# A latent attention's order written out tile by tile, and a recurrence's group norms emitted after it

## The chip, the cores and the metric

One core of one Trainium2 chip runs the whole program. The time is device microseconds of one execution, the median of three. "Before" is the kernel without the change. The engines are TensorE (PE, with its weight loads as PEld), VectorE (DVE), ScalarE (ACT), GpSimd (POOL) and SyncE (SP).

## The reference, cut to what matters

The program is two decoder layers and a further block. Each layer projects its input, runs a two-way RWKV recurrence and a latent attention on the same projection, mixes both, and runs a mixture of experts. Of a layer, the change touches these two parts (T is 1040 tokens: 16 meta tokens and 1024):

```python
# latent attention: 4 heads, 128 + 64 wide keys, 128 wide values
s = jnp.einsum('bqhd,bkhd->bhqk', qn, k_nope) + jnp.einsum('bqhd,bkd->bhqk', qp, k_pe)
p = jax.nn.softmax(s.astype(jnp.float32) * scale, axis=-1)
out = jnp.einsum('bhqk,bkhd->bqhd', p, v)
# end of the recurrence: group norm over each head of 64, bonus, gate
mu = jnp.mean(y, -1, keepdims=True)
var = jnp.mean(jnp.square(y - mu), -1, keepdims=True)
yn = ((y - mu) * lax.rsqrt(var + RWKV_GN_EPS)).reshape(B, L, RW) * gn_g + gn_b
out = (yn + (bonus_f + bonus_b).reshape(B, L, RW)) * g
```

## The kernel before, in words

Matrix products keep fp32 accuracy by splitting each operand in a high and a low half (names ending in h and l) and adding three products: `split` (L251 on ScalarE, L252 on VectorE) makes the halves, `mm3` (L256 to L258) multiplies.

**`recur`** ends with nine calls of `r_post` (L985), one for the 16 meta rows and eight for 128 rows each. A row loads four arrays from HBM, adds on GpSimd (L996), takes the mean on VectorE (L1001, L1002), subtracts on GpSimd (L1003), squares on ScalarE (L1004), sums on VectorE (L1006), takes the root on ScalarE (L1007) and the reciprocal on VectorE (L1008), multiplies and adds on GpSimd (L1009, L1010) and VectorE (L1011 to L1013), gates on GpSimd (L1014) and stores the row (L1015). `mix_out`, after the attention, reads it. ScalarE's root and exponential use different tables, each change is an `ACT_TABLE_LOAD`. Its tiles (names q_...) have two buffers each.

**`mla`** makes the halves of the latent inputs and weights, then for head h `qk` (projections of q and k, split), `qk_rotary` (the rotary part `qs`, a copy on ScalarE, L1098, and a subtraction on VectorE, L1099) and, for each pair of heads, `values`. PSUM has two large tiles (`big`, three banks each) and two of one bank (tag t). A head's 9 query tiles form four groups, [0,1,2], [3,4], [5,6], [7,8].

`scores` does one query tile: 15 matmuls (L1149), the row maximum (L1151, L1152), the exponentials with their sums (L1155, L1157), nine transposes of the probabilities `Pm` in three sets, key tiles 1 to 4, 5 to 8, and tile 0 (L1163), each set with a copy from PSUM on ScalarE (L1166), and a cast and a subtraction on VectorE (L1169, L1170) into `pth` and `ptl`. `output` multiplies a group's probabilities by the values (27 matmuls, `ops`), and copies to `m_ot` (L1179); with a head's last group it also transposes back (L1186), writes `y_att` (L1189) and squares and sums (`m_sq`, `s_ss`, L1192 to L1194).

Nothing here is in a manual order: the Tile framework's scheduler lays out each engine's instructions from the program order and its own costs, so the rows of `r_post` and the tiles of `mla` are interleaved by it on all engines. Only the loop of `recur` runs in a written order (`manual_schedule`). `mla` is called with the recurrence's work ahead of it in program order.

Of the kernel before, what the change touches and what calls it, by code (L numbers as in the profile page):

```python
# [10 lines left out]
F32 = mybir.dt.float32  # L11
# [161 lines left out]
class K:  # L173
# [521 lines left out]
    def recur(self, li, S):  # L695
        nc, tc, I = self.nc, self.tc, self.I
        with ExitStack() as es:
# [6 lines left out]
            R = dict(li=li, S=S)  # L704
# [9 lines left out]
            R.update(ap=ap, bp=bp, mp=mp, st=pool("r_s", 2), tp=pool("r_t", 2), qp=pool("q_t", 2, side="right"),  # L714
# [12 lines left out]
            qc = pool("q_c", 1, side="right")  # L727
            R["gb"] = self.bcast(qc, I["rwkv_gn_g"][li], RW, "gn_g")
            R["bb"] = self.bcast(qc, I["rwkv_gn_b"][li], RW, "gn_b")
# [71 lines left out]
            for i in range(9):  # L801
                self.r_post(R, i)
# [219 lines left out]
    def mla(self, li, p, S, Y):  # L1022
# [7 lines left out]
        with ExitStack() as es:  # L1030
# [48 lines left out]
            def qk(h):  # L1079
# [6 lines left out]
                c3(lambda q, c, n: self.split(qh[:, c:c + n], ql[:, c:c + n], ps[:, q, :n]))  # L1086
                kh = hp.tile([128, T], F32R, name="kh")
# [3 lines left out]
                return [(qh, kh), (qh, kl), (ql, kh)]  # L1091
# [10 lines left out]
            def values(pr):  # L1102
# [3 lines left out]
                wv = [w[:, pr, 1].rearrange("p h f -> p (h f)") for w in (wkh, wkl)]  # L1106
                for i, (c, n) in enumerate(TT):
                    vp = pst.tile([128, 512], F32, name="vps", tag="t")
                    self.mm3(vp[:n, :256], ckh[:, c:c + n], ckl[:, c:c + n], wv[0], wv[1], True, True)
                    self.split(vh[:n, i], vl[:n, i], vp[:n, :256])  # L1110
                return vh, vl

            QK, V = {0: qk(0)}, {0: values(0)}
            with self.tpool(name="m_r", bufs=1) as lp:
# [15 lines left out]
                for pr in range(2):  # L1130
# [5 lines left out]
                    if pr == 0:  # L1136
                        QK[0] += qk_rotary(0)
# [4 lines left out]
            def scores(h, i, terms, pth, ptl, o):  # L1142
# [4 lines left out]
                for q, (c, m) in enumerate(self.KC):  # L1147
                    for z, (l, r) in enumerate(terms):
# [5 lines left out]
                sm = S["sums"][:, h, i]  # L1154
                nc.scalar.activation(P[:n, 0:696].rearrange("p (a b) -> p a b", a=2), sp[:n, 0:2, :348], AF.Exp,  # L1155
                                     scale=rq[:n, i:i + 1], bias=mx[:n], accum_out=sm[:n, 0:1])
                nc.scalar.activation(P[:n, 696:T], sp[:n, 2, 4:348], AF.Exp, scale=rq[:n, i:i + 1], bias=mx[:n],  # L1157
                                     accum_out=sm[:n, 1:2])
                for kts in ((1, 2, 3, 4), (5, 6, 7, 8)) + ((0,),):
# [5 lines left out]
                    kn, z, k0 = TT[kts[0]][1], len(kts), TT[kts[0]][0]  # L1165
                    nc.scalar.activation(P[:kn, k0:k0 + z * n].rearrange("p (z n) -> p z n", z=z), pt[:kn, :z, :n], AF.Copy)  # L1166
# [5 lines left out]
            def output(h, ot, w0, W, pth, ptl, last):  # L1172
# [7 lines left out]
                if not last:  # L1180
                    return
# [9 lines left out]
                sq = tp.tile([128, 8, 128], F32, name="m_sq", bufs=1)  # L1191
                nc.scalar.activation(sq, rows, AF.Square)  # L1192
                nc.vector.tensor_reduce(S["ss"][:, h, 1:9], sq, AX.X, ALU.add)
                nc.scalar.activation(sq[:NM, 0], rp[:NM, 1024:1152], AF.Square, accum_out=S["ss"][:NM, h, 0:1])  # L1194

            due = None
            for h in range(4):
                ot = None
                for z, grp in enumerate(groups):
                    w0 = TT[grp[0]][0]  # L1200
                    W = TT[grp[-1]][0] + TT[grp[-1]][1] - w0
                    pth = ep.tile([128, 9, 272], F32R, name="pth")
                    ptl = ep.tile([128, 9, 272], F32R, name="ptl")
                    for i in grp:
                        scores(h, i, QK[h], pth, ptl, TT[i][0] - w0)
                    if due:
                        output(*due)
# [1315 lines left out]
```

## Time and profile before

| | us |
|---|---|
| before, median of 3 | 4390.69 |
| lowest to highest | 4386.52 to 4403.39 |
| the profiled execution | 4402.54 |
| its span | 4400.7 |
| mean granted clock, share of 2.4 GHz | 0.903 |

The span is the time between the first and the last instruction on the core. A busy time is the sum over an engine's instructions, weight loads (PEld) run beside matmuls. "Idle before" is the time in which the engine stood still ahead of an instruction, put down to what ended it.

### The profile page before, as it was taken

What the parts mean: (1) busy time and instruction counts of PE and PEld (TensorE: products, weight loads), DVE (VectorE), ACT (ScalarE), POOL (GpSimd) and SP (SyncE); (2) the same over time, 40 slices, a digit from 0 to 9 for tenths busy, and PEclk for the clock granted to TensorE, in tenths of its full rate; (3) what the DMA queues carried; (4) which work ended last, traced back from release to release, by engine and by line L of the source; (5) the groups of instructions that cost most, each with busy time, mean ns of one, the idle gap of its engine ahead of it and who ended that gap; (6) DMA issues with size and microseconds to landing.
All of it is one profiled execution on the core that took longest, in us unless ns stands there. A gap on an engine that the chain in (4) does not pass through costs nothing. (4 is left out here: it accounts for less than half of the span.)

```text
span 4400.7 us, 68329 instructions
## 1 busy us (share of the span) xinstructions
PE 3830.7 (87%) x27155; PEld 3157.1 (72%) x27155; DVE 2767.7 (63%) x4684; ACT 1869.7 (42%) x3033; POOL 988.2 (22%) x719
## 2 busy tenths in 40 slices
PE   7888897899699688897887896997898889999998
PEld 7677676786576476776776775765786677888786
DVE  7763777757698757627668577997644753333354
ACT  4323445542387543233555532876424522111232
POOL 2331124201242243311233012331422410000000
PEclk9788798999799887886988997999998899999999
DMA  4446663113499833447641043998521121111232
GB/s 154 101 129 183 160 161 108 37 54 128 160 345 346 300 102 101 115 143 172 165 125 58 1 172 131 340 335 309 181 73 29 53 97 58 48 48 43 90 126 81
DMA packets 384153, 611.94 MB, mean 139 GB/s; under 512 B 50467, under 2 KB 217602, under 8 KB 381762
## 3 DMA queue, kind: packets, MB, share of 16 engines
q1 hardware_dynamic: 278402, 485.38, 35.3%
q10 hardware_dynamic: 85200, 70.97, 5.4%
q0 software_dynamic: 20224, 51.15, 3.7%
q8 instruction: 216, 3.54, 0.3%
q14 instruction: 111, 0.91, 0.1%
HBM read 491.65 MB, written 123.45 MB: 140 GB/s over the span
## 5 line engine op out<-in xcount | busy, mean ns | idle before, releaser
L252 DVE TENSOR_TENSOR w13l<-xw,w13h 128x1024 fp32r<-128x1024 f32 x248 | 296.4, 1220 | 57.5 <-ACT w13h L251 53.9
L251 ACT ACTIVATE w13h<-xw 128x1024 fp32r<-128x1024 f32 x256 | 267.4, 1058 | 130.3 <-PE x_hp L258 76.6
L256 PE MATMUL pp_ps<-T_hi,pw_hi 128*128 128x348 f32 x912 | 309.7, 340 | 8.7 <-ACT T_hi L1752 2.9
L257 PE MATMUL pp_ps<-T_lo,pw_hi 128*128 128x348 f32 x912 | 305.4, 335 | 1.4 <-DVE T_lo L1757 1.3
L258 PE MATMUL pp_ps<-T_hi,pw_lo 128*128 128x348 f32 x912 | 304.3, 334 | 0.0
L2414 PE MATMUL f_mm<-F_hi,f_wh 128*128 128x512 f32 x704 | 222.8, 398 | 1.7 <-ACT F_hi L251 1.7
L2414 PE MATMUL f_mm<-F_lo,f_wh 128*128 128x512 f32 x704 | 222.6, 397 | 0.0
L2414 PE MATMUL f_mm<-F_hi,f_wl 128*128 128x512 f32 x704 | 222.3, 397 | 0.0
L256 PE MATMUL x_hp<-w13h,x_h 128*96 128x512 f32 x512 | 208.5, 407 | 0.1
L257 PE MATMUL x_hp<-w13l,x_h 128*96 128x512 f32 x512 | 204.7, 400 | 0.0
L258 PE MATMUL x_hp<-w13h,x_l 128*96 128x512 f32 x512 | 204.0, 398 | 0.0
L256 PEld LDWEIGHTS pp_ps<-T_hi,pw_hi 128*128 128x128 f32 x912 | 179.8, 197 | 21.8 <-issue 7.8
L257 PEld LDWEIGHTS pp_ps<-T_lo,pw_hi 128*128 128x128 f32 x912 | 179.8, 197 | 5.1 <-DVE T_lo L1757 2.6
L287 POOL TENSOR_TENSOR g_x<-g_x,g2g 128x1024 f32<-128x1024 f32 x6 | 14.3, 2385 | 750.4 <-ACT g_x L284 750.4
L258 PEld LDWEIGHTS pp_ps<-T_hi,pw_lo 128*128 128x128 f32 x912 | 179.5, 197 | 3.0 <-issue 3.0
L252 DVE TENSOR_TENSOR f_wl<-F_raw,f_wh 128x1024 fp32r<-128x1024 f32 x44 | 53.7, 1221 | 203.2 <-ACT f_wh L251 203.2
L251 ACT ACTIVATE f_wh<-F_raw 128x1024 fp32r<-128x1024 f32 x44 | 46.4, 1060 | 307.0 <-PE f_mm L2414 301.4
L1616 POOL DMA_INDIRECT d_y<-x_o,r_idx x64 | 102.8, 1606 | 312.1 <-DVE x_al L252 288.8
L825 PE MATMUL aa<-ar_p,bk_p 64*128 64x128 f32 x1088 | 134.0, 376 | 40.2 <-DVE A L827 33.6
L2414 PEld LDWEIGHTS f_mm<-F_hi,f_wh 128*128 128x128 f32 x704 | 133.1, 189 | 34.4 <-ACT F_hi L251 2.0
L2414 PEld LDWEIGHTS f_mm<-F_lo,f_wh 128*128 128x128 f32 x704 | 132.7, 189 | 32.8 <-DVE F_lo L252 0.6
L2414 PEld LDWEIGHTS f_mm<-F_hi,f_wl 128*128 128x128 f32 x704 | 132.9, 189 | 32.4
(630 smaller groups left out, 11221.3 us busy)
## 6 DMA issues: line engine op xcount, KB each, us to landing
xw<-in_moe_w SPq DMA_DIRECT2D x256, 512.0 KB
xw<-in_moe_w SPq DMA_DIRECT2D x64, 1024.0 KB
wd_raw<-in_w_down SPq DMA_DIRECT2D x44, 512.0 KB
pw_raw<-in_w_in SPq DMA_DIRECT2D x36, 512.0 KB
d_AR<-AR ACTq DMA_DIRECT2D x32, 544.0 KB
d_BK<-BK ACTq DMA_DIRECT2D x32, 544.0 KB
ar_p<-d_AR SPq DMA_DIRECT2D x68, 256.0 KB
bk_p<-d_BK SPq DMA_DIRECT2D x68, 256.0 KB
```

Of the source, the lines that this page charges most:

```text
L251: nc.scalar.activation(hi, src, AF.Copy)
L252: (lo_eng or nc.vector).tensor_tensor(lo, src, hi.bitcast(F32), ALU.subtract)
L256: mm(out, wh, xh, start=first, stop=False)
L257: mm(out, wh, xl, start=False, stop=False)
L258: mm(out, wl, xh, start=False, stop=last)
L287: e1.tensor_tensor(out[:n], out[:n], gb[:n], ALU.mult)
L825: nc.tensor.matmul(aa[d][:, h - z], bk[q, h], ar[q, h], start=True, stop=True)
L1616: nc.gpsimd.indirect_dma_start(out=y2[:, :], out_offset=bass.IndirectOffsetOnAxis(ap=si, axis=0), in_=y, in_offset=None, bounds_check=2 * ...
L2414: nc.tensor.matmul(p[:, j], a[:, k], b[:, k, 512 * j:512 * j + 512], start=st, stop=sp)
```

## The change

`recur` no longer emits the rows: it returns nine calls, and `mla` emits them at its end, after the attention, in program order. Their pool `q_t` has one buffer for each tile instead of two and lives until the end of `mla`; the group norm's weights lie in it from the start of `recur`.

`mla` runs 36 query tiles in 38 turns under a manual order for TensorE, ScalarE and VectorE. Turn t emits the scores of tile t, the transposes and splits of tile t−1 (`turned`), the exponentials of tile t, and then an output that is due (`output`, and `back` at a head's end), a piece of `values(1)` or of the next head's `qk`. Key tile 0 comes first in `turned`, and its halves are made straight from PSUM. `m_sq` is squared and summed in two halves. The rows, emitted behind, are still placed by the scheduler: GpSimd's and SyncE's instructions are free, and it sets the rows' VectorE and ScalarE instructions into the written order.

```diff
-    def recur(self, li, S):
+    def recur(self, li, S, qs):
-            R = dict(li=li, S=S)
+            R = dict(li=li, S=S, qp=qs)
+            R["gb"] = self.bcast(qs, I["rwkv_gn_g"][li], RW, "gn_g")
+            R["bb"] = self.bcast(qs, I["rwkv_gn_b"][li], RW, "gn_b")
...
-            R.update(ap=ap, bp=bp, mp=mp, st=pool("r_s", 2), tp=pool("r_t", 2), qp=pool("q_t", 2, side="right"),
+            R.update(ap=ap, bp=bp, mp=mp, st=pool("r_s", 2), tp=pool("r_t", 2),
...
-            qc = pool("q_c", 1, side="right")
-            R["gb"] = self.bcast(qc, I["rwkv_gn_g"][li], RW, "gn_g")
-            R["bb"] = self.bcast(qc, I["rwkv_gn_b"][li], RW, "gn_b")
...
-            for i in range(9):
-                self.r_post(R, i)
+            return iter([lambda i=i: self.r_post(R, i) for i in range(9)])
...
-    def mla(self, li, p, S, Y):
+    def mla(self, li, p, S, Y, rows):
...
+                yield None
...
-                return [(qh, kh), (qh, kl), (ql, kh)]
+                yield None
+                yield [(qh, kh), (qh, kl), (ql, kh)] + qk_rotary(h)
...
+                    if i in (4, 8):
+                        yield
+            QK, V = {}, {}
+            Q = qk(0)
+            for z in range(2):
+                next(Q)
+            for z in values(0):
+                pass
...
-                        QK[0] += qk_rotary(0)
+                        QK[0] = next(Q)
...
-            def scores(h, i, terms, pth, ptl, o):
+            def scores(h, i, terms):
...
+                def exps():
+                    sm = S["sums"][:, h, i]
+                    nc.scalar.activation(P[:n, 0:696].rearrange("p (a b) -> p a b", a=2), sp[:n, 0:2, :348], AF.Exp,
+                                         scale=rq[:n, i:i + 1], bias=mx[:n], accum_out=sm[:n, 0:1])
+                    nc.scalar.activation(P[:n, 696:T], sp[:n, 2, 4:348], AF.Exp, scale=rq[:n, i:i + 1], bias=mx[:n],
+                                         accum_out=sm[:n, 1:2])
+                return P, exps
-                for kts in ((1, 2, 3, 4), (5, 6, 7, 8)) + ((0,),):
+            def turned(P, i, pth, ptl, o):
+                n = TT[i][1]
+                for kts in ((0,), (1, 2, 3, 4), (5, 6, 7, 8)):
                     pt = pst.tile([128, 4, 128], F32, name="ptp", tag="t")
                     for z, kt in enumerate(kts):
                         kc, kn = TT[kt]
                         nc.tensor.transpose(pt[:kn, z, :n], P[:n, kc:kc + kn], self.ident[:n, :n])
                     kn, z, k0 = TT[kts[0]][1], len(kts), TT[kts[0]][0]
+                    if z == 1:
+                        ph, pl = pth[:kn, 0, o:o + n], ptl[:kn, 0, o:o + n]
+                        nc.scalar.activation(ph, pt[:kn, 0, :n], AF.Copy)
+                        nc.vector.tensor_tensor(pl, pt[:kn, 0, :n], ph.bitcast(F32), ALU.subtract)
+                        continue
...
-            def output(h, ot, w0, W, pth, ptl, last):
+            def output(h, ot, w0, W, pth, ptl):
...
-                if not last:
-                    return
+            def back(h, ot):
...
-                sq = tp.tile([128, 8, 128], F32, name="m_sq", bufs=1)
-                nc.scalar.activation(sq, rows, AF.Square)
-                nc.vector.tensor_reduce(S["ss"][:, h, 1:9], sq, AX.X, ALU.add)
+                sq = tp.tile([128, 4, 128], F32, name="m_sq", bufs=1)
+                for z in (0, 4):
+                    nc.scalar.activation(sq, rows[:, z:z + 4], AF.Square)
+                    nc.vector.tensor_reduce(S["ss"][:, h, 1 + z:5 + z], sq, AX.X, ALU.add)
...
-            due = None
-            for h in range(4):
-                ot = None
-                for z, grp in enumerate(groups):
-                    w0 = TT[grp[0]][0]
-                    W = TT[grp[-1]][0] + TT[grp[-1]][1] - w0
-                    pth = ep.tile([128, 9, 272], F32R, name="pth")
-                    ptl = ep.tile([128, 9, 272], F32R, name="ptl")
-                    for i in grp:
-                        scores(h, i, QK[h], pth, ptl, TT[i][0] - w0)
-                    if due:
-                        output(*due)
-                    if h == 2 and z == 0:
-                        V[1] = values(1)
-                    if z == 0:
-                        ot = tp.tile([128, T], F32, name="m_ot", bufs=1)
-                    if z == 1 and h < 3:
-                        QK[h + 1] = qk(h + 1) + qk_rotary(h + 1)
-                    due = (h, ot, w0, W, pth, ptl, z == 3)
-            output(*due)
+            jobs = [(h, z, i) for h in range(4) for z, grp in enumerate(groups) for i in grp]
+            ot, cur, due, prev, value = None, None, [], None, iter(())
+            with self.tc.manual_schedule(engines={mybir.EngineType.PE, mybir.EngineType.Activation, mybir.EngineType.DVE}):
+                for t in range(len(jobs) + 3):
+                    exps = None
+                    if t < len(jobs):
+                        h, z, i = jobs[t]
+                        P, exps = scores(h, i, QK[h])
+                    now, done = due, []
+                    due = []
+                    if prev:
+                        Pp, (hp_, zp, ip) = prev
+                        grp = groups[zp]
+                        if ip == grp[0]:
+                            w0 = TT[ip][0]
+                            W = TT[grp[-1]][0] + TT[grp[-1]][1] - w0
+                            if zp == 0:
+                                ot = tp.tile([128, T], F32, name="m_ot", bufs=1)
+                            cur = [ep.tile([128, 9, 272], F32R, name=nm) for nm in ("pth", "ptl")]
+                        turned(Pp, ip, *cur, TT[ip][0] - w0)
+                        if ip == grp[-1]:
+                            due = [(hp_, ot, w0, W, *cur)]
+                            last = zp == 3
+                    if exps:
+                        exps()
+                    for job in now:
+                        output(*job)
+                        if job[0] == 1 and job[2] == TT[7][0]:
+                            value = values(1)
+                        if job[2] == TT[7][0]:
+                            back(*job[:2])
+                    next(value, None)
+                    if t < len(jobs):
+                        if h < 3 and z == 1 and i == groups[1][0]:
+                            Q = qk(h + 1)
+                        if h < 3 and (z, i) in ((1, groups[1][0]), (1, groups[1][1]), (2, groups[2][0])):
+                            got = next(Q)
+                            if got:
+                                QK[h + 1] = got
+                        prev = (P, jobs[t])
+                    else:
+                        prev = None
+            for row in rows:
+                row()
...
-                self.recur(li, S)
+                qs = ExitStack()
+                rows = self.recur(li, S, qs.enter_context(self.tpool(name="q_t", bufs=1)))
...
-                    self.mla(li, p, S, Y)
+                    self.mla(li, p, S, Y, rows)
+                    qs.close()
```

The order of instructions shows it at three places. First TensorE, early in layer 0's loop, where transposes (`ptp`) and score matmuls (`ms`) meet. Before:

```order
L1163 MATMUL ptp<-ident,Pm 16x16
L1163 MATMUL ptp<-ident,Pm 128x128 x4
L1149 MATMUL ms<-kh,qh 128x348
L1149 MATMUL ms<-kl,qh 128x348
L1149 MATMUL ms<-kh,ql 128x348
L1149 MATMUL ms<-kph,qs 128x348
L1149 MATMUL ms<-kpl,qs 128x348
L1163 MATMUL ptp<-ident,Pm 128x128 x4
L1163 MATMUL ptp<-ident,Pm 16x128
L1149 MATMUL ms<-kh,qh 128x348
```

Now, in a turn whose output (`ops`) follows:

```order
L1157 MATMUL ms<-kh,ql 128x348
L1157 MATMUL ms<-kph,qs 128x348
L1157 MATMUL ms<-kpl,qs 128x348
L1178 MATMUL ptp<-ident,Pm 16x128
L1178 MATMUL ptp<-ident,Pm 128x128 x8
L256 MATMUL ops<-pth,vh 128x272
L257 MATMUL ops<-ptl,vh 128x272
```

The score matmuls that lay between the transposes of the first and the second four key tiles are gone; nine transposes follow each other, tile 0 first, and the output follows them.

Second VectorE, at the start of layer 0's loop (`qs` is the rotary part of q, `q_...` are the rows). Before:

```order
L1012 TENSOR_TENSOR q_y_6782<-q_y_6782,gn_g 128x512
L1099 TENSOR_TENSOR qs<-qpe_7016,qs 64x1040
L1134 TENSOR_TENSOR qr<-ms,sin 128x348
L1134 TENSOR_TENSOR qr<-ms,sin 128x346 x2
L1013 TENSOR_TENSOR q_y_6782<-q_y_6782,q_v 128x512
L1099 TENSOR_TENSOR qs<-qpe_7016,qs 64x1040
L252 TENSOR_TENSOR vl<-vps,vh 128x256
L1151 TENSOR_REDUCE mx<-ms 16x1
L1151 TENSOR_REDUCE mx<-ms 128x1
L1152 TENSOR_TENSOR mx<-mx,s_nrq 16x1
L1152 TENSOR_TENSOR mx<-mx,s_nrq 128x1
L1001 TENSOR_REDUCE q_mu<-q_y_6807 128x8
```

Now:

```order
L1100 TENSOR_TENSOR qs<-qpe_6786,qs 64x1040
L1142 TENSOR_TENSOR qr<-ms,sin 128x348
L1142 TENSOR_TENSOR qr<-ms,sin 128x346 x2
L252 TENSOR_TENSOR vl<-vps,vh 128x256
L1159 TENSOR_REDUCE mx<-ms 16x1
L1160 TENSOR_TENSOR mx<-mx,s_nrq 16x1
L1159 TENSOR_REDUCE mx<-ms 128x1
L1160 TENSOR_TENSOR mx<-mx,s_nrq 128x1
L1185 TENSOR_TENSOR ptl<-ptp,pth 16x16
L1190 CAST pth<-Pm 128x4x16
```

The second `qs`, which is head 1's, has left the place ahead of the first maxima `mx`; so has the row of 128 that stood there.

Third ScalarE, at the first row inside the loop. Before:

```order
L1166 ACTIVATE Pm<-ptp 128x64 x2
L1004 ACTIVATE q_y_6808<-q_y_6807 128x512
L1007 ACT_TABLE_LOAD
L1007 ACTIVATE q_vr<-q_vr,eps_gn 128x8
L1166 ACTIVATE Pm<-ptp 16x16
L1166 ACTIVATE Pm<-ptp 128x512
L1155 ACT_TABLE_LOAD
L1155 ACTIVATE Pm,s_sums<-ms,mx,s_rq 128x696
L1157 ACTIVATE Pm,s_sums<-ms,mx,s_rq 128x344
L1166 ACTIVATE Pm<-ptp 128x512
```

Now:

```order
L1184 ACTIVATE pth<-ptp 16x16
L1187 ACTIVATE Pm<-ptp 128x64 x2
L1165 ACTIVATE Pm,s_sums<-ms,mx,s_rq 128x696
L1167 ACTIVATE Pm,s_sums<-ms,mx,s_rq 128x344
L1003 ACTIVATE q_y_9355<-q_y_9354 128x512
L1184 ACTIVATE pth<-ptp 16x128
L1187 ACTIVATE Pm<-ptp 128x512 x2
L1006 ACT_TABLE_LOAD
L1006 ACTIVATE q_vr<-q_vr,eps_gn 128x8
L1165 ACT_TABLE_LOAD
L1165 ACTIVATE Pm,s_sums<-ms,mx,s_rq 128x696
L1167 ACTIVATE Pm,s_sums<-ms,mx,s_rq 128x344
```

A row's square (`q_y`) and root (`q_vr`) still lie between copies and exponentials, with two table loads for it; the copies of one tile now stand together.

## Rows read from the trace of the kernel before

**Rows 1.** The page's first part: busy us (share of the span) and instructions.

```profile
PE 3830.7 (87%) x27155; PEld 3157.1 (72%) x27155; DVE 2767.7 (63%) x4684; ACT 1869.7 (42%) x3033; POOL 988.2 (22%) x719
```

**Rows 2.** Timeline, layer 0: start us, us, operation, idle before it.

```profile
710.80 0.32 PE L1149 MATMUL ms<-kh,qh 128*16 128x348 f32 x1 [1.10 <-DVE qpe L1134]
715.36 6.93 DVE L1099 TENSOR_TENSOR qs<-qpe,qs 64x1040 fp32r<-64x1040 f32 x1
722.66 2.37 DVE L1151 TENSOR_REDUCE mx<-ms 16x1 f32<-16x1044 f32 x2
725.18 1.28 ACT L1155 ACT_TABLE_LOAD   x1 [13.98 <-DVE mx L1152]
727.55 1.11 PE L1163 MATMUL ptp<-ident,Pm 16*128 16x16 f32 x8 [8.96 <-ACT Pm L1155]
...
841.85 1.25 DVE L1151 TENSOR_REDUCE mx<-ms 128x1 f32<-128x1044 f32 x1 [0.31 <-PE ms L1149]
...
995.14 0.19 ACT L1194 ACTIVATION_READ_ACCUMULATOR m_sq<-ms 16x1 f32 x1
```

**Rows 3.** Timeline, layer 1: first score matmul, last square.

```profile
2279.05 0.32 PE L1149 MATMUL ms<-kh,qh 128*16 128x348 f32 x1
...
2554.28 0.19 ACT L1194 ACTIVATION_READ_ACCUMULATOR m_sq<-ms 16x1 f32 x1
```

**Rows 4.** Tile `mx`, layers 0 and 1: duration ns min/median/max, first, last start.

```profile
L1151 DVE TENSOR_REDUCE mx<-ms x36: 1222/1245/1247, 722.7 to 972.6; 128x1 f32<-128x1044 f32 x32, 16x1 f32<-16x1044 f32 x4
L1151 DVE TENSOR_REDUCE mx<-ms x36: 1225/1245/1247, 2286.4 to 2533.3; 128x1 f32<-128x1044 f32 x32, 16x1 f32<-16x1044 f32 x4
```

**Rows 5.** Table of stretches: us; engines' busy us; clock; DMA share; GB/s.

```profile
680.00:710.00 30.00, 23.64 (x126) 23.09 (x126) 24.61 (x42) 15.03 (x28) 11.54 (x11) 0.83 0.45 136
728.00:842.00 114.00, 92.25 (x517) 83.89 (x516) 92.10 (x170) 70.86 (x146) 46.92 (x41) 0.83 0.23 65
842.00:973.00 131.00, 117.21 (x782) 105.94 (x782) 79.94 (x178) 70.18 (x175) 0.74 (x2) 0.96 0.00 1
973.00:997.00 24.00, 17.54 (x117) 14.67 (x114) 11.02 (x28) 10.75 (x23) 0.66 (x4) 0.91 0.85 294
2306.00:2410.00 104.00, 77.61 (x469) 69.44 (x468) 83.70 (x152) 60.75 (x125) 46.92 (x36) 0.89 0.22 66
```

**Rows 6.** Groups by line, 842 to 973 us: busy us, mean ns; idle before.

```profile
L1151 DVE TENSOR_REDUCE mx<-ms 128x1 f32<-128x1044 f32 x20 | 24.9, 1244 | 17.3 <-PE ms L1149 17.1
L1166 ACT ACTIVATE Pm<-ptp 128x512 f32<-128x512 f32 x35 | 19.9, 593 | 20.8 <-PE ptp L1163 20.6
L1169 DVE CAST pth<-Pm 128x512 fp32r<-128x512 f32 x34 | 14.2, 419 | 15.7 <-ACT Pm L1166 15.3
```

**Rows 7.** Waits, 842 to 973 us: engine, line, releaser: us, times, longest.

```profile
DVE ql L252 <- ACT qh L251: 2.5, 1, 2.5
PE ptp L1163 <- ACT Pm L1166: 2.5, 7, 1.1
PE ops L256 <- ACT Pm L1166: 2.2, 6, 0.6
```

**Rows 8.** Groups by line, 728 to 842 us, VectorE, ScalarE, GpSimd in turn.

```profile
L1169 DVE CAST pth<-Pm 128x512 fp32r<-128x512 f32 x24 | 14.9, 636 | 3.2 <-ACT Pm L1166 3.1
L1011 DVE TENSOR_TENSOR q_y<-q_y,q_vr 128x512 f32<-128x512 f32 x7 | 5.5, 788 | 0.1
L1008 DVE RECIPROCAL q_vr<-q_vr 128x8 f32<-128x8 f32 x7 | 1.4, 196 | 3.1 <-ACT q_vr L1007 3.1
...
L1007 ACT ACT_TABLE_LOAD x7 | 9.0, 1283 | 0.8 <-POOL q_y L1014 0.7
L1004 ACT ACTIVATE q_y<-q_y 128x512 f32<-128x512 f32 x7 | 4.4, 623 | 4.4 <-POOL q_y L1003 4.4
...
L1014 POOL TENSOR_TENSOR q_y<-q_y,q_g 128x512 f32<-128x512 f32 x7 | 10.1, 1442 | 20.3 <-DVE q_y L1013 16.6 <-DVE q_mu L1002 3.7
L995 POOL DMA_DIRECT2D q_y<-d_y x11 | 7.0, 635 | 13.1 <-DVE q_vr L1006 9.6 <-DMA d_yr<-q_y 3.5
```

More of the change, by code (lines that the diff above doesn't have):

```diff
@@ L1106, in values @@
                 wv = [w[:, pr, 1].rearrange("p h f -> p (h f)") for w in (wkh, wkl)]
+                V[pr] = vh, vl
                 for i, (c, n) in enumerate(TT):
@@ L1110, in values @@
                     self.split(vh[:n, i], vl[:n, i], vp[:n, :256])
-                return vh, vl
-            QK, V = {0: qk(0)}, {0: values(0)}
+                    if i in (4, 8):
[6 more added lines that the diff above has]
+                pass
             with self.tpool(name="m_r", bufs=1) as lp:
@@ L1153, in scores @@
                 P = tp.tile([128, T], F32, name="Pm", bufs=3)
[L1154 to L1158, printed above, removed]
-                for kts in ((1, 2, 3, 4), (5, 6, 7, 8)) + ((0,),):
+                def exps():
[8 more added lines that the diff above has]
+                for kts in ((0,), (1, 2, 3, 4), (5, 6, 7, 8)):
                     pt = pst.tile([128, 4, 128], F32, name="ptp", tag="t")
```

## The prediction

> **What bounds the kernel now.** I read the page's first part, then the table of stretches, then the instructions of one tile, then the waits. TensorE is busy 87% of the span [rows 1], and the change touches only the attention `mla` and the last nine steps of the recurrence, twice each (two layers). So everything is read from those two places. The timeline's first score matmul and the last square of layer 0 stand at 710.80 and 995.14, those of layer 1 at 2279.05 and 2554.28 [rows 2, 3]: 284.5 and 275.4 us, 6.5 and 6.3% of the span.
>
> Inside these stretches there are three regimes. First a start: from the first score matmul to the first row maximum (722.66 in layer 0, 2286.36 in layer 1) 11.9 and 7.3 us pass. Then 35 intervals between the first and the last of 36 row maxima, 250.0 us to 972.6 and 246.9 us to 2533.28 [rows 3, 4]. Then a tail of 22.7 and 21.2 us. In the middle the table of stretches [rows 5] splits: 842 to 973 us holds no group norms: 20 full maxima [rows 6] and two short ones, whose 21 intervals take 130.8 us (from 841.85 [rows 2] to 972.6), 6.23 us a tile, with TensorE busy 117.21 of 131 us and VectorE 79.94. 728 to 842 us holds seven group-norm rows and only 14 intervals in 119.2 us, 8.5 us a tile, with TensorE at 92.25 of 114 and VectorE at 92.10. Layer 1's stretch of the second kind, 2306 to 2410 us, reads like layer 0's. So without group norms TensorE is the limit and waits little; with them all engines share a tangle.
>
> The start of layer 0 has a stall of its own [rows 2]: VectorE's second `qs` (head 1's) takes 6.93 us while GpSimd works; behind it stand `vl` and the first two row maxima, ScalarE then sits 13.98 us before its table load and TensorE 8.96 us before the first transposes.
>
> **The change, part by part.** I price TensorE's chain, since in the new order it is the engine that every iteration comes back to.
>
> *Fixed order without group norms.* TensorE's own work per tile stays: 117.21 us over 21 tiles are 5.58 us. What changes is what it waits for. Now one iteration is 15 score matmuls, nine transposes, perhaps an output. Before, score matmuls of a later tile lay between the transposes of key tiles 1 to 4 and those of 5 to 8, as the printed order shows; now nothing does, and the second four need the PSUM tile that ScalarE's copy of the first four must have left. That copy takes 593 ns [rows 6], and it stands behind the copy of the 16-row tile. Before, this kind of wait cost 2.5 us over 7 times, 0.36 on average and 1.1 at the longest [rows 7]; these are my two bounds. I take 0.9, near the longest, because with nothing between the whole chain shows: the copy's 0.59 and about 0.3, an estimate between that and the 1.1, for the last transpose to come out and the copy to start. In an iteration with an output, its first matmul waits in the same way for the copy of key tiles 5 to 8; before 2.2 us in 6 times, 0.6 at the longest [rows 7]. There are 16 outputs for 36 tiles, so I add 0.9 × 16/36 = 0.4. The projections of heads 1 to 3 now go in as three pieces each, and ScalarE's and VectorE's halves of their splits alternate: the row before has VectorE waiting 2.5 us for the first of them [rows 7], and I take 3.7 for a head's set, 11 us over 36 tiles or 0.3. Sum: 5.58 + 0.9 + 0.4 + 0.3 = 7.2 us a tile against 6.23. VectorE's work (79.94 us over 22 tiles, 3.6 a tile) and ScalarE's (70.18, 3.2) [rows 5] fit under that, so neither is the bound; the cast of the 16-row key tile that goes from VectorE counts nothing there.
>
> *Group norms.* The same nine rows come with the same instructions and their place in the loop hardly moves: row 0 before it, rows 1 to 8 inside (before rows 0 and 1 stood ahead). One row's price on VectorE is seven steps, from 788 ns (`q_y` by `q_vr`) to 196 ns (the reciprocal), 3.95 us together; on ScalarE a square of 0.62 and two table loads of 1.283, 3.2 us [rows 8]. Lower bound 0 (it falls into their idle time); upper bound 7.1 (one after the other on the path). I take 2.6, the two table loads, because they are ahead of exponentials that TensorE's next transposes need: 8 × 2.6 = 21 us. To this come 4 us for VectorE running slower beside GpSimd (a large cast takes 636 ns there [rows 8] and 419 without it [rows 6]: 5 us for 24 casts, most of it in the path). Sum for the middle: 35 × 7.2 + 25 = 277 us, against 250 and 247: +27 and +30.
>
> *The chain of a row.* One buffer instead of two means that the loads of row i+1 wait until row i is stored. GpSimd already waits 3.5 us in all for such a store [rows 8], and SP's and GpSimd's queues carry no other work here that the loop needs before its end. So I cost the single buffer at nothing by itself; its cover is that rows stand two iterations apart, and if that goes the price is rival 2.
>
> *Start.* Head 1's `qs` moves from ahead of the loop to iteration 5, where the work of five tiles is past and the next head is four iterations off. So no long `qs` stands before the first maximum. I take 5.5 us for the start (15 short matmuls at the low clock, one wait for `qs`): −6 in layer 0, −2 in layer 1. *Ahead of the loop* VectorE is busy 24.61 of 30 us [rows 5]; row 1's seven instructions leave it, 3.95 us, and I take −4 a layer (bounds 0 and −5, since GpSimd's help ends too).
>
> *Tail.* From the last maximum: transposes 1.9 with their wait, an output 4, again transposes 1.9, an output 4, then output transposes, copy, squares in two halves, about 6: 18 to 19, against 22.7 and 21.2. I take −3. The loads of `mix_out`'s weights may go out earlier, but nothing waited for them, so 0.
>
> **Sum.** Layer 0: 27 − 6 − 4 − 3 = +14; layer 1: 30 − 2 − 4 − 3 = +21; together +35, less about 4 that I allow because some of the waits fall under a row's stall anyway: +31. On the profiled execution's 4402.5 us that is 4433.5; that execution lay 11.8 us above the median 4390.7, so I predict 4390.7 + 31 = **4422**.
>
> **The clock.** TensorE was granted 0.96 of its 2.4 GHz between 842 and 973 us, but 0.83 between 728 and 842, and 0.89 in layer 1's stretch with group norms [rows 5]: there it dropped to 1.2 GHz for parts. If the new stretches without group norms came at 0.89, TensorE's 5.58 us would grow by 0.44 us, times 44 tiles 19 us more. I leave this out of the sum, since the tail shows 0.91 with many waits, and keep it for the upper end. The Trainium skill, "TensorE: Matmul & The Clock Gate", Part 1, says that the throttled state is the default and that activity releases it, which speaks against an order that makes TensorE wait in each iteration; going by it the 19 us would be due, 4441. The trace agrees in that its stretches with more waits have the lower clock, 0.83 against 0.96.
>
> **Rivals.**
> 1. *Faster: the transposes' wait stays at its old price.* If ScalarE is always free when the first four transposes come out, and weight loads of the next hide the start, the wait is the 0.36 of before and not 0.9. Over 52 waits a layer that takes off 28 us, twice 28 = 56: 4366. It would cease to be slower from a wait of 0.6. For it: 7 such waits averaged that. Against: those had matmuls of other tiles between. Chance 0.24.
> 2. *Slower by more: rows hold the queues.* If a row's VectorE or ScalarE step stands in the fixed order before its input has come from GpSimd or from a store, the whole loop stands. Speaking for it: in one such stretch VectorE waited 3.1 us for ScalarE's `q_vr`. Against: the long waits were GpSimd's, 16.6 us for VectorE's `q_y` [rows 8], so its results were early. With 5.1 us a row (half-way from the 3.1 of the sum to 7.1): 16 rows × 2.0 more is +32, 4454; at 7.1 it is 4486. The Trainium skill, "PSUM — Partial Sum Buffer", "Engine vs sequencer instructions", calls these engines' queues strict FIFO; nothing behind passes a waiting step. Chance 0.18.
> 3. *No change: the rows are hidden.* If rows fall into time in which VectorE and ScalarE idle (ScalarE was busy 70.86 of 114 us), the 25 us a layer go: 4422 − 50 = 4372. Chance 0.2. This is also where it ends if the new order is only the old one written out in effect.
>
> **How the numbers follow.** Forecast 0.38, its own range 4400 to 4445. A measurement here tells about 0.5%, 22 us, from no change: faster is under 4369, slower over 4412. Faster: 0.18 of rival 1 and 0.06 of rival 3 (both at once, or less at the clock), 0.24. Same: 0.06 of rival 1, 0.13 of rival 3, 0.11 of the forecast, 0.30. Slower: 0.27 of the forecast, 0.18 of rival 2, a rest of 0.01: 0.46. The range takes in most of rival 1 and the middle of rival 2: 4352 to 4465.
>
> **What would show it.** In the changed profile: maxima 7.2 us apart where no group norms lie; TensorE's transposes waiting for ScalarE's copy over 30 times, about 0.9 us each; the first maximum some 5.5 us behind the first score matmul; a tail of 18 to 19 us; 3 us a row on top. Maxima at most 6.6 us apart, or the rows without effect on their spacing, make the forecast wrong towards faster; a table load or `q_vr` reciprocal waiting several us in every row, towards slower.

## The result, and the profile after

The changed kernel took 4433.15 us (4426.66 to 4439.29, 4 runs) against 4388.67 for the kernel before in the same comparison: ratio 1.0094, 95% interval 1.0067 to 1.0121, 44 us more. The profiled execution took 4431.16 us with a span of 4429.3, close to that median; the one of before, 4402.54, lay above its own.

In the trace the difference lies in the two attention loops. From the first projection to the first matmul of `mix_out` layer 0 took 322.7 us, before 314.3, and layer 1 330.6, before 304.8: 34 us in all. These two stretches before, then now (the view of [rows 5]; behind a stretch's length stands TensorE's busy time with the count of its matmuls, and the third number from the end is its granted clock, a mean of time at 1.2 and at 2.4 GHz as a share of 2.4):

```profile
682.10:996.40 314.30, 257.13 (x1570) 232.26 (x1570) 220.99 (x430) 167.41 (x371) 71.06 (x64) 0.89 0.20 62
2250.80:2555.60 304.80, 248.75 (x1571) 222.59 (x1571) 214.49 (x430) 166.60 (x371) 75.53 (x64) 0.92 0.20 62
```

```profile
678.70:1001.40 322.70, 253.08 (x1571) 228.54 (x1571) 210.28 (x398) 175.28 (x377) 72.64 (x67) 0.91 0.21 66
2251.00:2581.60 330.60, 260.46 (x1571) 235.04 (x1571) 209.73 (x398) 175.12 (x377) 72.01 (x67) 0.88 0.21 65
```

The matmuls are the same but for one record. What is left of a stretch when TensorE's busy time is taken off is the time in which it stands: 57.2 and 56.1 us before, 69.6 and 70.1 now, 12.4 and 14.1 more. The busy time itself fell by 4.1 us in layer 0, where the granted clock rose from 0.89 to 0.91, and rose by 11.7 in layer 1, where the clock fell from 0.92 to 0.88. So TensorE stands longer by about the same in both layers, and that layer 1 lost 26 us and layer 0 only 8 goes with the clock.

The row maxima show where the time went; 36 of them, first and last start (the view of [rows 4]):

```profile
L1159 DVE TENSOR_REDUCE mx<-ms x36: 1225/1240/1247, 708.5 to 983.3; 128x1 f32<-128x1044 f32 x32, 16x1 f32<-16x1044 f32 x4
L1159 DVE TENSOR_REDUCE mx<-ms x36: 1226/1238/1247, 2281.1 to 2563.5; 128x1 f32<-128x1044 f32 x32, 16x1 f32<-16x1044 f32 x4
```

274.8 us lie between first and last in layer 0 and 282.4 in layer 1, against 250.0 and 246.9. The start is short now. Second half of `qs`, first score matmul, first maximum, layer 0 (the view of [rows 2]):

```profile
704.18 2.21 DVE L1100 TENSOR_TENSOR qs<-qpe,qs 64x1040 fp32r<-64x1040 f32 x1 [0.45 <-ACT qs L1099]
...
705.36 0.32 PE L1157 MATMUL ms<-kh,qh 128*16 128x348 f32 x1
...
708.55 1.23 DVE L1159 TENSOR_REDUCE mx<-ms 16x1 f32<-16x1044 f32 x1 [0.42 <-PE ms L1157]
```

3.2 us from the first matmul to the first maximum, where 11.9 passed before; only one `qs` is left ahead of the first maximum. The tail ends earlier too, the last instruction of the squares in the two layers stands at:

```profile
1000.08 0.18 ACT L1216 ACTIVATION_READ_ACCUMULATOR m_sq<-ms 16x1 f32 x1
...
2580.26 0.18 ACT L1216 ACTIVATION_READ_ACCUMULATOR m_sq<-ms 16x1 f32 x1
```

That is 16.8 us behind the last maximum in both, against 22.5 and 21.0. So start and tail won 14.4 us in layer 0 and 8.3 in layer 1, and the middle lost 24.9 and 35.5.

What a turn without an output looks like once the rows are over; timeline of layer 0, start and duration in us, TensorE's transposes, the maximum, and ScalarE's copies:

```profile
970.85 0.71 PE L1178 MATMUL ptp<-ident,Pm 128*16 128x128 f32 x5
971.05 1.25 DVE L1159 TENSOR_REDUCE mx<-ms 128x1 f32<-128x1044 f32 x1 [0.54 <-PE ms L1157]
971.15 0.27 ACT L1184 ACTIVATE pth<-ptp 16x128 fp32r<-16x128 f32 x1 [0.30 <-PE ptp L1178]
971.65 0.60 ACT L1187 ACTIVATE Pm<-ptp 128x512 f32<-128x512 f32 x1 [0.23 <-PE ptp L1178]
972.30 0.66 PE L1178 MATMUL ptp<-ident,Pm 128*128 128x128 f32 x4 [0.75 <-ACT Pm L1187]
```

Five transposes, then TensorE stands 0.75 us until ScalarE has copied the first four key tiles, then the other four; the next maximum comes 4.33 us after the last. This repeats within two hundredths in each such turn. Over the whole stretch without rows, 889 to 983 us, the waits are (the view of [rows 7]: engine, line, releaser: us in all, times, longest):

```profile
PE ptp L1178 <- ACT Pm L1187: 12.0, 14, 2.2
```

14 times in 14 tiles, 0.86 us each; before it was 7 times in 21 tiles, 0.36 each. Between the first and the last maximum of layer 0 this wait of TensorE's was, before and now:

```profile
PE ptp L1163 <- ACT Pm L1166: 6.5, 14, 1.4
```

```profile
PE ptp L1178 <- ACT Pm L1187: 32.1, 34, 3.0
PE vps L256 <- DVE vl L252: 10.4, 3, 6.7
PE ptp L1178 <- ACT Pm L1165: 8.8, 6, 2.3
PE ops L256 <- ACT Pm L1187: 6.2, 10, 0.7
```

The other three lines are its longest further waits now: the value matmuls for a subtraction, the transposes for the exponential, the outputs for a copy. In the stretch with rows, 709 to 850 us, VectorE's reciprocals wait for the root as well:

```profile
DVE q_vr L1007 <- ACT q_vr L1006: 6.8, 5, 2.3
```

The table of stretches (the view of [rows 5]), two stretches with rows and the one without:

```profile
709.00:850.00 141.00, 109.34 (x660) 98.73 (x660) 100.73 (x183) 86.03 (x176) 50.59 (x46) 0.89 0.20 58
2281.00:2420.00 139.00, 107.62 (x618) 97.11 (x617) 93.61 (x170) 79.81 (x163) 48.96 (x44) 0.85 0.21 59
...
889.00:983.00 94.00, 80.15 (x537) 73.02 (x536) 55.69 (x108) 49.49 (x116) 0.58 (x1) 0.96 0.18 67
```

TensorE is busy 85% in the last where it was busy 89% in [rows 5], and the granted clock is the same 0.96; with rows it is 0.89 and 0.85.

One place shows a row in the way of the queues. VectorE and TensorE at the last row of layer 0, while `values(1)` is due:

```profile
862.51 0.69 DVE L1000 TENSOR_REDUCE q_mu<-q_y 128x8 f32<-128x512 f32 x1 [3.09 <-POOL q_y L995]
...
869.61 0.69 DVE L1012 TENSOR_TENSOR q_y<-q_y,q_v 128x512 f32<-128x512 f32 x1
870.22 0.74 DVE L252 TENSOR_TENSOR vl<-vps,vh 16x256 fp32r<-16x256 f32 x2
...
870.67 0.58 PE L256 MATMUL vps<-wkh,ckh 128*128 128x256 f32 x1 [6.73 <-DVE vl L252]
```

VectorE stands 3.09 us until GpSimd has added the row, goes through the row's steps, and only at 870.22 reaches the subtraction for `vl` that TensorE's next value matmuls wait for, 6.73 us. Only a part of this wait is the row's. In the changed kernel without rows (below) TensorE waits at the same place, because the subtraction also stands behind the squares of the head's end:

```profile
899.71 0.58 PE L256 MATMUL vps<-wkh,ckh 128*128 128x256 f32 x1 [4.52 <-DVE vl L252]
```

So 4.5 of the 6.7 us come without any row, and about 2.2 are the row's.

### The profile page after: what moved, and what is told of

Read it like the earlier page. It is cut to its first block, busy times and chain, and to the rows that moved or that the text cites. A ratio compares the mean times of both kernels' runs of the same rounds, so it can differ in the third digit from the quotient of the medians.

```text
span 4429.3 us, 68240 instructions
## 1 busy us (share of the span) xinstructions
PE 3836.0 (87%) x27155; PEld 3164.4 (71%) x27155; DVE 2757.1 (62%) x4620; ACT 1886.2 (43%) x3045; POOL 985.6 (22%) x719
## 4 chain that ended last, share of the span: by engine, by line
PE 37%; DVE 4%; ACT 3%; DMA 3%; issue 2%; POOL 1%; SPq 0%; ACTq 0%; DVEq 0%; POOLq 0%; another core or an unknown queue 0%
PE f_mm L2463 11%; PE a_ft L2035 3%; DMA xw<-in_moe_w 2%; PE g_mm L256 2%; PE g_mm L257 2%; PE g_mm L258 2%; PE ms L1157 1%; PE x_hp L256 1%; PE x_hp L257 1%; PE x_hp L258 1%; PE o_mm L256 1%; PE ptp L1178 1%; PE o_mm L257 1%; PE o_mm L258 1%; PE d_s L2238 1%
## 5 line engine op out<-in xcount | busy, mean ns | idle before, releaser
L2463 PE MATMUL f_mm<-F_hi,f_wl 128*128 128x512 f32 x704 | 222.3, 397 | 0.0
L257 PE MATMUL x_hp<-w13l,x_h 128*96 128x512 f32 x512 | 204.8, 400 | 0.0
L1178 PE MATMUL ptp<-ident,Pm 128*128 128x128 f32 (+3 forms) x648 | 98.7, 280 | 84.3 <-ACT Pm L1187 65.3
```

The source lines that it names most:

```text
L257: mm(out, wh, xl, start=False, stop=False)
L1178: nc.tensor.transpose(pt[:kn, z, :n], P[:n, kc:kc + kn], self.ident[:n, :n])
L2463: nc.tensor.matmul(p[:, j], a[:, k], b[:, k, 512 * j:512 * j + 512], start=st, stop=sp)
```

## The experiments

**The wait covered.** The last five score matmuls of a tile move between the two sets of transposes:

```diff
+                part((0, 1))
...
+                def rest():
+                    part((2,))
+                    nc.vector.tensor_reduce(mx[:n], sp[:n, :, :348], AX.XY, ALU.max)
...
+                    if kts[0] == 1 and rest:
+                        rest()
```

> The changed kernel with one thing moved: the transposes of key tile 0 and key tiles 1 to 4 come ahead of the last five score matmuls of the next tile, those of 5 to 8 behind them. Theory (TensorE waits about 0.9 us in each turn for ScalarE's copy of key tiles 1 to 4): five matmuls, 0.8 us, cover that wait, maxima without outputs come 3.6 us apart instead of 4.33, and 36 turns twice make 50 to 60 us less: 4370 to 4385. Rival (ScalarE, VectorE or the rows set the pace, the wait is only where it shows): it comes back ahead of key tile 0's transposes, less than 15 us are won, 4418 to 4435.

4384.65 us (10 runs; ratio to the kernel before 0.9989, 0.9976 to 1.0001): 48 us less than the changed kernel, at the upper end of the range; in the profiled executions 36 of them lie in the two attentions, 617.1 against 653.3 us. The total came out as in the theory, but not by its path, so the fit is partly luck: a turn without output takes 4.10 us instead of 4.33, not 3.6, and one with output 7.1 instead of 7.9. In layer 0's middle TensorE now waits 7.6 us for the copy, but 17.4 for the exponentials, 8.8 before, and 8.2 for a subtraction: part of the wait came back ahead of other transposes, as the rival had it. Maxima, exponentials and transposes of that kernel, layer 0:

```profile
953.56 1.25 DVE L1167 TENSOR_REDUCE mx<-ms 128x1 f32<-128x1044 f32 x1 [0.66 <-PE ms L1160]
954.84 0.16 DVE L1168 TENSOR_TENSOR mx<-mx,s_nrq 128x1 f32<-128x1 f32 x1
955.03 0.93 ACT L1172 ACTIVATE Pm<-ms,mx,s_rq 128x696 f32<-128x696 f32 x1 [0.38 <-DVE mx L1168]
955.96 0.63 ACT L1174 ACTIVATE Pm<-ms,mx,s_rq 128x344 f32<-128x344 f32 x1
956.11 0.71 PE L1185 MATMUL ptp<-ident,Pm 128*16 128x128 f32 x5 [0.55 <-ACT Pm L1172]
957.66 1.25 DVE L1167 TENSOR_REDUCE mx<-ms 128x1 f32<-128x1044 f32 x1 [0.35 <-PE ms L1160]
```

The maximum and its scaling end at 955.0, the exponentials follow at once, and the transposes stand 0.55 us for the first of them: one tile's own chain now sets the turn.

**One more tile in flight**, to see whether that chain is the limit: turn t turns tile t−2.

```diff
-                        prev = (P, jobs[t])
-                    else:
-                        prev = None
+                        hist.append((P, jobs[t]))
+                    prev = hist.pop(0) if hist and t >= 1 else None
```

> The kernel with the split transposes, with one more tile in flight: turn t turns tile t-2 instead of t-1. Theory (what holds turns without output at 4.10 us there is the chain of one tile: last five score matmuls, maximum, exponentials, transposes): those turns fall to 3.9 us, where VectorE's own 3.9 us of work is the next limit, those with an output from 7.1 to 6.8; 4360 to 4380. Rival (VectorE or the rows already set 4.10): same turns, 4380 to 4395.

4379.08 us (ratio 0.9975, 0.9964 to 0.9986). The total stands where the two expected ranges meet and does not tell them apart; the turns do. Those without output fall to 3.69, lower than the 3.9 expected, so the chain was the limit; those with output rise to 7.36 instead of falling to 6.8, which was wrong. The middles are 252.8 and 250.8:

```profile
L1167 DVE TENSOR_REDUCE mx<-ms x36: 1222/1223/1246, 705.3 to 958.1; 128x1 f32<-128x1044 f32 x32, 16x1 f32<-16x1044 f32 x4
L1167 DVE TENSOR_REDUCE mx<-ms x36: 1222/1223/1246, 2258.6 to 2509.4; 128x1 f32<-128x1044 f32 x32, 16x1 f32<-16x1044 f32 x4
```

**The rows left out**, in both kernels. A row then only loads one array and stores it:

```diff
-        nc.gpsimd.tensor_tensor(y0[:n], y0[:n], y1[:n], ALU.add)
...
-        nc.gpsimd.tensor_tensor(y0[:n], y0[:n], g[:n], ALU.mult)
         nc.scalar.dma_start(S["yr"][c0:c0 + n, :], y0[:n])
```

> The changed kernel whose nine rows only load one array and store it: the group norm, bonus and gate of the recurrence are left out. Theory: a row costs about 3 us in the loop, 25 us a layer, so 4433 - 50 = 4383, range 4370 to 4395. Rival 1 (rows hold the queues, 5 us a row or more): 4355 or less. Rival 2 (rows hidden): above 4420.

> The kernel before whose nine rows only load one array and store it: group norm, bonus and gate left out. Theory: in the kernel before the rows cost more than in the changed one, by the spacing of maxima 2.3 us for 14 tiles and the stall at the start, some 35 to 40 us a layer, so 4389 - 75 = 4314, range 4300 to 4330. Rival (rows cost the same 25 us in both orders): 4339, range 4332 to 4350.

The totals, 4598.71 and 4541.8, miss every range and say nothing of the loops: in the changed kernel without rows the recurrence ahead of layer 0's loop ran some 50 us longer and what follows the second attention 128 us longer. The experts work on other data there; the first recurrence does not, and why it ran longer stays open. The loops can be read: of the last ten intervals of a layer, which hold no row in the changed kernel, at least nine come out within 0.03 us with the rows and without. The changed kernel without rows, then the kernel before without rows:

```profile
L1137 DVE TENSOR_REDUCE mx<-ms x36: 1233/1245/1246, 760.8 to 1007.8; 128x1 f32<-128x1044 f32 x32, 16x1 f32<-16x1044 f32 x4
L1137 DVE TENSOR_REDUCE mx<-ms x36: 1232/1245/1246, 2350.0 to 2594.8; 128x1 f32<-128x1044 f32 x32, 16x1 f32<-16x1044 f32 x4
```

```profile
L1129 DVE TENSOR_REDUCE mx<-ms x36: 1223/1245/1248, 758.0 to 976.1; 128x1 f32<-128x1044 f32 x32, 16x1 f32<-16x1044 f32 x4
L1129 DVE TENSOR_REDUCE mx<-ms x36: 1223/1245/1248, 2327.3 to 2549.6; 128x1 f32<-128x1044 f32 x32, 16x1 f32<-16x1044 f32 x4
```

247.0 and 244.8 us against 218.1 and 222.3. Per interval that is 7.06 and 6.99 us in the written order, 6.23 and 6.35 in the scheduler's: the new tile code in its written order costs 29 and 23 us with no row there. The rows add 27.8 and 37.6 in the changed kernel and 31.8 and 24.6 between the first and last maximum of the kernel before, where its slow starts come on top. From the first projection to `mix_out`, the changed kernel without rows and then the kernel before without rows:

```profile
731.80:1025.80 294.00, 241.66 (x1570) 219.28 (x1570) 168.95 (x335) 147.07 (x343) 6.90 (x8) 0.94 0.13 41
2319.50:2612.90 293.40, 240.63 (x1571) 218.26 (x1571) 168.95 (x335) 147.19 (x343) 6.90 (x8) 0.94 0.13 41
```

```profile
726.30:998.40 272.10, 237.48 (x1570) 214.47 (x1570) 167.19 (x367) 142.23 (x339) 6.84 (x8) 0.96 0.11 36
2296.40:2571.90 275.50, 242.68 (x1570) 219.15 (x1570) 167.09 (x367) 142.04 (x339) 6.83 (x8) 0.94 0.11 35
```

By these the tile code in its order costs 22 and 18 us, since less is left for its tail, and the rows 28.7 and 37.2 in the changed kernel, 42.2 and 29.3 in the kernel before. Of the rows' price in the changed kernel 17.3 and 17.4 us are time in which TensorE stands; the rest, 11.4 and 19.8, is the same matmuls at a lower clock, 0.94 without rows, 0.91 and 0.88 with them. In the kernel before it is 22.6 and 23.2 us of standing, and 19.7 and 6.1 of busy time.

**No table loads.** A copy in the place of the rows' root:

```diff
-        nc.scalar.activation(vr[:n], vr[:n], AF.Sqrt, scale=1.0 / 64, bias=self.eps["gn"][:n])
+        nc.scalar.activation(vr[:n], vr[:n], AF.Copy, scale=1.0 / 64)
```

> The changed kernel with a copy in place of the root in the group norm's rows, so that ScalarE changes no table in the loop; the root and its epsilon are left out. Only the loops are read, since the experts' routing changes. Theory (the price of a row is its two table loads, 2.6 us): 8 rows, 21 us less between the first and the last maximum, 274.8 and 282.4 become 254 and 262 within 5. Rival (the rows cost through the waits on VectorE, GpSimd and their loads): at least 265 and 273.

```profile
L1159 DVE TENSOR_REDUCE mx<-ms x36: 1227/1236/1246, 703.4 to 963.6; 128x1 f32<-128x1044 f32 x32, 16x1 f32<-16x1044 f32 x4
L1159 DVE TENSOR_REDUCE mx<-ms x36: 1226/1236/1246, 2248.0 to 2509.5; 128x1 f32<-128x1044 f32 x32, 16x1 f32<-16x1044 f32 x4
```

260.2 and 261.5 us in the one execution that there is (4374.56 us), 14.6 and 20.9 less, the first a microsecond beyond the range, the second in it: half of the rows' price in both layers and a little more comes with the table loads, 1.8 to 2.6 us a row. TensorE stands 9.7 and 6.2 us less; its busy time falls by 4.9 and 14.7, at a clock of 0.93 in both where it was 0.91 and 0.88.

**The parts of the change, each alone.** First the changed kernel with the manual order around the tiles taken off:

```diff
-            with self.tc.manual_schedule(engines={mybir.EngineType.PE, mybir.EngineType.Activation, mybir.EngineType.DVE}):
+            if True:
```

> The changed kernel with the manual order around the 36 tiles taken off: same program order, rows behind with one buffer each, but the scheduler sets the order again. Theory (the written order costs, the rows' place does not): back to the kernel before within 15 us, 4375 to 4405, and 6.2 to 6.6 us a tile where no rows lie. Rival (the rows with one buffer, or emitted behind, cost): stays at 4420 or more, or loses at the end of the attention where the rows then stand.

4352.05 us (4 runs; ratio to the kernel before 0.9906, 0.9883 to 0.9929). Both sides were too high: this beats both kernels. Maxima, and the transposes' wait between them in layer 0:

```profile
L1159 DVE TENSOR_REDUCE mx<-ms x36: 1194/1238/1248, 708.4 to 945.2; 128x1 f32<-128x1044 f32 x32, 16x1 f32<-16x1044 f32 x4
L1159 DVE TENSOR_REDUCE mx<-ms x36: 1194/1238/1246, 2253.2 to 2490.2; 128x1 f32<-128x1044 f32 x32, 16x1 f32<-16x1044 f32 x4
```

```profile
PE ptp L1178 <- ACT Pm L1187: 10.1, 13, 2.5
```

236.8 and 237.0 us between first and last maximum with all rows in it; TensorE waits for the copy 13 times, 10.1 us, where it was 34 times and 32.1 in the manual order. Then three more kernels fill the table; the first is the kernel before with only the rows' part (and squares in halves), the second the new tile code in the scheduler's order with the rows where they were, the third the manual order with the rows where they were.

> The kernel before with the rows' part of the change alone: rows emitted at the end of the attention, one buffer each, and (for space) squares in two halves; old tile code, scheduler's order. Theory A (what the changed kernel gains in the scheduler's order comes from the rows: a tile's work now goes ahead of theirs): 4355 to 4370. Theory B (it comes from the new tile code: key tile 0 first and straight from PSUM, the next head's work in pieces): 4380 to 4395.

> The changed kernel's tile code in the scheduler's order, with the rows emitted ahead of the attention and two buffers, as before. Theory A (the gain is the rows'): 4380 to 4395. Theory B (the gain is the tile code's): 4350 to 4370.

> The changed kernel's tile code in its manual order, with the rows ahead and two buffers as before. Theory (the written order costs some 26 us a layer without rows, whatever the rows do): slower than the kernel before by 40 to 80 us, 4430 to 4470. Rival (one buffer and the place behind make the manual order slow): 4385 to 4410.

| median us | rows ahead, two buffers | rows behind, one buffer |
|---|---|---|
| old tile code, scheduler's order | 4385 to 4390 (before) | 4383.94 |
| new tile code, scheduler's order | 4392.86 | 4352.05 |
| new tile code, manual order | 4445.38 | 4433.15 (changed) |

The manual order costs 53 us in the left column and 81 in the right, so in either place of the rows; this part is as expected. In the profiled executions the two attentions take 55 and 64 us more by it, of which TensorE stands 45 and 46. Of the 81 us the two edits above win back 54; where the other 27 lie stays open. The gain of the free order is neither theory's: the rows' part alone gives −1.5 us (ratio 0.999, 0.998 to 0.9999), the tile code alone loses 7 (1.0015, 1.0005 to 1.0025), together they gain 36. One more run splits the tile code, by putting key tile 0 back to the end and through a copy:

```diff
-                for kts in ((0,), (1, 2, 3, 4), (5, 6, 7, 8)):
+                for kts in ((1, 2, 3, 4), (5, 6, 7, 8), (0,)):
...
-                    if z == 1:
+                    if False:
```

> The kernel with the new tile code in the scheduler's order and the rows behind, but with the transposes as before: key tiles 1 to 4, 5 to 8, then 0, and tile 0 through ScalarE's copy, a cast and a subtraction. Theory A (its gain over the rows' part alone comes from key tile 0, which frees VectorE of a cast and lets the copies go without waiting for a subtraction): back to 4375 to 4392. Theory B (it comes from the program order of the new loop, transposes one turn late and the next head in pieces): stays at 4348 to 4362.

4367.23 us (ratio 0.9942, 0.9919 to 0.9965), between the two: by the medians 15 us are key tile 0's and 17 the loop's program order. The profiled executions bear out the first, 605.6 us in the two attentions against 589.4, and of the second only 4.6, from 610.2; where the rest of it lies isn't shown. Why neither shows with the rows ahead stays open; a guess not tried is that a free order can use the freed time only where a tile's work goes ahead of a row's.

Last, the table loads in the free order:

> The same replacement of the root by a copy in the kernel whose tile code stands in the scheduler's order with the rows behind. Theory (in that order other work of TensorE covers a table load): 236.8 and 237.0 us between first and last maximum fall by under 8 us. Rival (a table load costs there what it costs in the manual order): by 15 us or more.

```profile
L1159 DVE TENSOR_REDUCE mx<-ms x36: 1180/1244/1247, 710.8 to 935.9; 128x1 f32<-128x1044 f32 x32, 16x1 f32<-16x1044 f32 x4
L1159 DVE TENSOR_REDUCE mx<-ms x36: 1195/1240/1246, 2231.7 to 2461.0; 128x1 f32<-128x1044 f32 x32, 16x1 f32<-16x1044 f32 x4
```

225.1 and 229.3 us (one execution, 4332.18 us), 11.7 and 7.7 less: the first between both, the second just within the theory. TensorE stands only 2.7 and 1.9 us less, where it was 9.7 and 6.2 in the manual order; the other 9.0 and 5.8 are its busy time, at a clock of 0.98 and 0.96 where it was 0.92 and 0.93. So the free order covers most of the standing, and what a table load still costs there goes with the clock.

## Why the prediction was right, point by point

The forecast was 31 us slower, range 4352 to 4465; measured were 44 us slower, 4433.

- *Fixed order without rows.* 7.2 us a tile against 6.23 was forecast; without rows it is 7.0 to 7.1 against 6.2 to 6.35, over all 35 intervals. In the changed kernel's own stretch without rows it is 6.7 (14 intervals from 889.37 us), since the long interval with `values(1)` lies ahead of it; there the kernel before, with a head's projections among its last 14, needs 7.0, so only whole loops compare. The wait for the copy was taken at 0.9 and over 30 times; it came 34 times in layer 0 at 0.94, 0.75 in a plain turn. The rival's price of 0.36 is out. The two smaller terms were too high: outputs wait 6.2 us in all where 14 stood, and the 11 us for projections don't show among TensorE's waits. The sum lacked the 10.4 us that the value matmuls wait.
- *Rows.* 25 us a layer was forecast, 27.8 and 37.6 came, so rival 3, hidden rows, is out. Taking the two table loads away won 14.6 and 20.9 us of the 21 taken for them, but only in part by the path that was thought of: TensorE's standing is 9.7 and 6.2 us of it, the rest is its busy time at another clock. What is left was sized at 4 us for GpSimd's slowing and is 13 to 17, of which 6 and 5 are again busy time (210.9 and 207.9 us between the maxima without table loads, 204.8 and 202.9 without rows); whether the others are the row steps on VectorE that wait in its queue (rival 2) was not measured. Rival 2 is there in a weak form: a reciprocal waits 1.4 us on average and 2.3 at the longest, not several us in every row. At the place shown above `vl` starts at 870.22, behind the last step of the row. The Trainium skill, "PSUM — Partial Sum Buffer", "Engine vs sequencer instructions", calls the queues of ScalarE, VectorE and GpSimd strict FIFO; by that `vl` can't pass the row's steps, and the trace agrees.
- *Start and tail.* 5.5 us of start forecast, 3.2 measured; a tail of 18 to 19, 16.8 measured. Both terms won more than taken, 14.4 and 8.3 us where 9 and 5 stood.
- *Ahead of the loop.* From the first projection to the first score matmul 2.0 and 1.4 us were won, not 4: row 1's seven steps left, but not all of them can have been on the path.
- *Sum.* Stretch by stretch +8 and +26 us, together 34 against 31, or 35 before the 4 that were allowed. That the sum came so near is partly luck. The 35 is 62 from the fixed order and the tail (35 × 0.97 − 3, twice) less 27 from rows, start and what lies ahead; by the kernels without rows it is 40 less 6. The order was priced 22 us too high and the gain at the rows 21 too high. That of the 44 us between the medians 10 lie outside these stretches can't be pinned down: in the two profiled executions the rest of the program went the other way, by 6 us, and the interval, 29 to 53 us, holds the 34.
- *Clock.* Left out of the sum. For the stretch without rows that was right: it was granted 0.96 as before, though TensorE waits in every turn. For the whole attentions it was not: the clock took 4 us off layer 0 and put 12 on layer 1, about 8 of the 34. Whether layer 1 always comes out lower, one profiled execution can't say. On the stretch without rows the Trainium skill, "TensorE: Matmul & The Clock Gate", Part 1, has the throttled state as the default that activity releases; by it 19 us more were held possible, and the trace does not show them there.

What the forecast did not see is that the change is two changes of opposite sign. Its rows and tile code are worth 36 us in the scheduler's order, and the manual order takes back 81.

## What to carry to other kernels

Before an order is written out, look at what the scheduler puts into each wait: here it laid score matmuls between two sets of transposes that share PSUM tiles, and the written order laid nothing, 0.75 us in a plain turn. Split a stretch into TensorE's standing and its busy time: here the standing grew by 12 and 14 us in two layers that lost 8 and 26. A written order needs other work at every point where TensorE depends on a copy of its own result, and enough tiles in flight that one tile's chain is not the turn. When a change has an ordering part and a code part, run the code part in the old ordering as well.

## What the runs showed of the hardware that was not expected

VectorE's durations for a plain tile add up to 3.9 us, yet with one more tile in flight the maxima come 3.69 us apart: neighbours on one engine overlap a little, and a sum of durations is no lower bound for a turn. `ACT_TABLE_LOAD` took 1.283 us each time and the exponential began right behind it; eight rows with two loads each cost the loop 14.6 and 20.9 us where the order was fixed, 11.7 and 7.7 where it was free, and more than half of all this is TensorE's busy time: without the loads it was granted 0.93 instead of 0.91 and 0.88, and 0.98 and 0.96 instead of 0.92 and 0.93. What standing does to the clock shows at 862 us: ahead of the 6.73 us in which TensorE stood it was granted 1.00 (855 to 866 us) and a value matmul took 0.28 us; behind them it was granted 0.50, 1.2 GHz, and the same matmul took 0.41.
